# Strassen forms of the tokens through two small buffers, mix loads two tiles ahead, norms among the last products of the down stage, last up projection part by part

## The chip, the cores and the metric

The kernel runs on one core of a Trainium2 chip. The metric is the device time of one execution in microseconds (us). The engines are named as the profile names them: PE (matmul; PEld is its weight load), ACT (ScalarE), DVE (VectorE), POOL (GpSimd) and SP (SyncE, which here only issues transfers; ACT and POOL issue some too). Each engine works through its own list in order and waits on semaphores of the others.

## The reference, cut to what matters

One layer of a streaming encoder for 1024 prompt frames and 8 x 16 sample frames, all float32:

```python
x = x + 0.5 * swiglu_1(rms_norm(x, norm_ff1))    # swiglu = (silu(x @ gate) * (x @ up)) @ down
proj = rms_norm(x, norm_mix) @ w_in              # D_MODEL = 1024, D_FF = 2816
mix = concat(rwkv7(proj[rwkv columns]), band_attention(proj[attention columns]))
x = x + mix @ w_out
x = x + 0.5 * swiglu_2(rms_norm(x, norm_ff2))
y = rms_norm(x, norm_final)                      # and the recurrent states and caches
```

## The kernel before, in words

The 1152 tokens are 9 tiles of 128. Every float32 product is made of three matmuls: each operand is split into a rounded part (ACT copies it) and the rest (POOL or DVE subtracts), called hi and lo here.

**Gate and up** (both feed-forwards) use a seven-product scheme on 2 x 2 blocks. `_x_forms` makes the token side, `F`: four transposed blocks x11, x12, x21, x22 of the normalised tokens, and three further sums of them, each as hi and lo, for two parts of the tokens: part 0 is tiles 0 to 4 (2 x 320 columns), part 1 is tiles 5 to 8 (2 x 256). It goes through c = 0..3, and all of one c stands in the buffer `bs` (one of it) until POOL has made the last lo. `_w_forms` makes the weight side, `frm`: seven forms, sums `cmb` by DVE, hi by ACT, lo by POOL. `_gate_up` runs for m = 0..10 a gate pass and an up pass; a pass is seven products t = 0..6 for both parts, 12 matmuls each. After m = 0 the parts alternate within each t; for m = 0 all of part 0 runs first. The PSUM banks are reused within a pass: the products t = 0, 1, 2 are copied to SBUF by ACT (`keep`, tile `r`, 5 buffers), and t = 3, 4, 5 read such a copy on DVE (`whole`, tile `y`). The results `hs` go to DRAM.

**Down** runs for m = 0..10: load `hr` (the hidden values), split to `h`, load and split two rows of blocks of the down weights, then 9 tiles x 12 matmuls into PSUM, which DVE adds to `x`. In the first feed-forward a generator `beside` makes attention bias tables between the m, on ACT's queue and DVE. Behind it `_norm_t` normalises and transposes in three groups of three tiles, and the projection (`_project`) starts.

**Output projection** (second half of the program): `_out_proj` per tile loads `mix` and `x`, splits `mix`, runs 48 matmuls, adds to x on DVE, stores x. The token norm follows (`_rms`, then a multiply by DVE), and the forms of part 0 after tile 4, those of part 1 after tile 8; then gate and up of the second feed-forward. The order on each engine is the order in which the code emits the instructions, which a scheduler of the framework has adjusted locally; pools of SBUF and PSUM buffers set which instruction waits for which.

Of the kernel before, what the change touches and what calls it, by code (L numbers as in the profile page):

```python
# [16 lines left out]
P = 128  # L17
# [48 lines left out]
def _constants(k, a):  # L66
    nc = k.nc
    c = k.const

    def t(shape, name):  # L70
        return c.tile(shape, F32, tag=name, name=name)

    k.ident = t([P, P], "ident")
    make_identity(nc, k.ident)
    k.mhalf = t([P, 8], "mhalf")
    nc.gpsimd.memset(k.mhalf, -0.5)

    k.vec = t([P, V_N], "vec")
    _vectors(k, ((V_FF1, 8, a["norm_ff1"][0]),), nc.sync)
# [116 lines left out]
def _norm_t(k, v0):  # L196

    nc = k.nc
    for g in range(3):
        xns = []  # L200
        for i in range(3 * g, 3 * g + 3):
            xn = k.w.tile([P, DM], F32, tag="raw", bufs=k.nraw, name="xn")
# [33 lines left out]
def _x_forms(k, part, xns, v0):  # L236


    nc = k.nc
    o, n = PARTS[part]  # L240
    F = k.F[part]
    for c in range(4):
        buf = k.bsp.tile([P, 7 * 320], F32, tag="bs", bufs=1, name="bs")
        bs = buf[:, :7 * n].rearrange("p (j n) -> p j n", n=n)
        for j, cc, half in ((0, c, 0), (5, c, 1), (1, c + 4, 0), (2, c + 4, 1)):
            ps = _bank(k, "ps_n")
            t = o + half * n
            end = t + n
            while t < end:
                i, r = divmod(t, P)  # L250
                m = min(P - r, end - t)
                at = t - o - half * n
                nc.tensor.transpose(ps[:, at:at + m], xns[i - o // P][r:r + m, cc * P:cc * P + P],
                                    k.ident[r:r + m, r:r + m])
                t += m
            gain = k.vec[:, v0 + cc:v0 + cc + 1]
            if j == 5:
                nc.vector.tensor_scalar(bs[:, j], ps[:, :n], gain, None, ALU.mult)
            else:
                nc.scalar.activation(bs[:, j], ps[:, :n], AF.Copy, scale=gain)  # L260
        sub = lambda out, a, b: nc.vector.tensor_tensor(bs[:, out], bs[:, a], bs[:, b], ALU.subtract)
        sub(3, 5, 0)
        sub(4, 2, 3)
        sub(5, 2, 5)
        sub(6, 1, 4)
        nc.scalar.activation(F[:, 0, :, c], bs, AF.Copy)
        hi = F[:, 0, :, c].bitcast(F32)
        nc.vector.tensor_tensor(F[:, 1, 0:3, c], bs[:, 0:3], hi[:, 0:3], ALU.subtract)
        nc.gpsimd.tensor_tensor(F[:, 1, 3:7, c], bs[:, 3:7], hi[:, 3:7], ALU.subtract)  # L269

# [32 lines left out]
def _gate_up(k, wg, wu, hd, m):  # L303

    nc = k.nc
    hs = [k.w.tile([P, 2, 2, n], F32, tag=f"hs{p}", bufs=1, name="hs") for p, (o, n) in enumerate(PARTS)]
    for up, w in enumerate((wg, wu)):
        forms = list(_w_forms(k, w[:, 2 * m * P:2 * m * P + 2 * P]))
        state = [{}, {}]
        turns = [(t, p) for t in range(7) for p in range(2)]  # L310
        if m == 0:
            turns = [(t, p) for p in range(2) for t in range(7)]
        for t, p in turns:
# [16 lines left out]
            def keep(name):  # L330
                r = k.w.tile([P, 320], F32, tag="r", bufs=5, name="r")[:, :n]
# [3 lines left out]
            def whole(r, f, half):  # L335
                h = hs[p][:, f, half]
                y = k.w.tile([P, 320], F32, tag="y", bufs=2, name="y")[:, :n]
# [27 lines left out]

def _gate_up_pool(k, s, pool):
    k.w = pool(s, "wa")
# [3 lines left out]
def _down(k, s, pool, wd, hd, xd, done, beside=()):  # L371
# [4 lines left out]
    k.nraw = 3  # L376
    k.w = pool(s, "wb")
    k.spl = (k.w, 4)
# [3 lines left out]
    for m in range(NF // 2):  # L382
# [6 lines left out]
        d = [_load_w(k, wd[f * P:(f + 1) * P, :], [DM], None) for f in (2 * m, 2 * m + 1)]  # L389
# [4 lines left out]
        next(beside, None)  # L394
# [29 lines left out]
def _project(k, a):  # L424
# [14 lines left out]
    def shifted(c):  # L439

        wt = _cols(k, w, c * P)
# [743 lines left out]
def _out_proj(k, ws, x, xd, i):  # L1185
# [3 lines left out]
    g, j = divmod(i, 3)  # L1189
    mix = k.w.tile([P, KC, P], F32, tag="raw", bufs=k.nraw, name="mix")  # L1190
    nc.sync.dma_start(mix, k.mixd[g][:, :, j * P:j * P + P])
    nc.sync.dma_start(x, xd[i])
    s = k.mxp.tile([P, 2, KC, P], F32R, tag="mx", bufs=2, name="mx")
    nc.scalar.activation(s[:, 0], mix, AF.Copy)
    nc.vector.tensor_tensor(s[:, 1], mix, s[:, 0].bitcast(F32), ALU.subtract)
    for n in range(2):
        b = slice(512 * n, 512 * n + 512)
        ps = k.psum.tile([P, 512], F32, tag="g", name="ps_wo")
        for c in range(KC):
            mm(ps, s[:, 0, c], ws[c][:, 0, b], start=c == 0, stop=False)  # L1200
            mm(ps, s[:, 0, c], ws[c][:, 1, b], start=False, stop=False)
            mm(ps, s[:, 1, c], ws[c][:, 0, b], start=False, stop=c == KC - 1)
        nc.vector.tensor_tensor(x[:, b], ps, x[:, b], ALU.add)
    nc.sync.dma_start(xd[i], x)
# [5 lines left out]
def tile_encoder_step(ctx: ExitStack, tc: tile.TileContext, *aps):  # L1210
# [7 lines left out]
    k.nraw, k.nspl, k.nt, k.nu = 3, 4, 20, 7  # L1218
# [27 lines left out]
    with ExitStack() as s_rw, ExitStack() as s_xg:  # L1246
# [3 lines left out]
        with ExitStack() as s:  # L1250
            fp = [pool(s, f"f{p}") for p in range(2)]
            k.F = [fp[p].tile([P, 2, 7, 4, n], F32R, name="F") for p, (o, n) in enumerate(PARTS)]
            _gate_up_pool(k, s, pool)
            with ExitStack() as sb:
                k.bsp = k.h = pool(sb, "bs")
                _constants(k, a)
                for p, tiles in enumerate((range(5), range(5, 9))):
                    xns = []
# [140 lines left out]
```

## Time and profile before

| | |
|---|---|
| median of 3 runs | 2731.88 us (2724.52 to 2738.44) |
| the profiled execution | 2736.82 us, its span in the profile 2735.0 us |
| busy share of the span | PE 89%, PEld 80%, DVE 41%, ACT 33%, POOL 40% |
| clock of TensorE granted over the span | 0.937 |
| idle time of PE | 293.7 us (span less 2441.3 busy) |

In rows of a timeline the first number is the start, the second the duration of the group in us, and in brackets stands how long the engine sat idle before and what ended that. In rows of windows the numbers are the length and then the busy time of each engine. Matmul durations overlap: the pace is read from the starts.

### The profile page before, as it was taken

The page shows a single profiled execution, that of the slowest core. Times are in us where ns is not written, and L with a number is a line of the kernel's source. Part 1 is how long each engine was busy: PE and PEld are TensorE (multiplying, and loading weights), DVE is VectorE, ACT ScalarE, POOL GpSimd, SP SyncE. Part 2 cuts the span into 40 slices and gives each one's busy share as a digit, 9 for nine tenths or more (in the row PEclk, how much of TensorE's full clock was granted, in tenths as well). Part 3 has the DMA queues.
Part 4 walks back from the last instruction along what each step waited for, and adds up shares of the span by engine and source line. Part 5 has one row for each costly group of instructions (what it writes and reads, how often), then busy time and mean ns, then how long its engine had stood idle before and what let it go on. Part 6 is the DMA issues. An engine that isn't in the chain of part 4 may idle for free. (4 is left out here: it accounts for less than half of the span.)

```text
span 2735.0 us, 43547 instructions
## 1 busy us (share of the span) xinstructions
PE 2441.3 (89%) x17416; PEld 2178.8 (80%) x17416; DVE 1127.3 (41%) x2315; ACT 915.3 (33%) x1887; POOL 1093.0 (40%) x966
## 2 busy tenths in 40 slices
PE   3899999988999899999979996666699999979998
PEld 2899999976887799988856664444599999978887
DVE  4322222216555344577746554132422222215556
ACT  4333333311112344334126666121333333321112
POOL 4545454524441344334034432020555555534442
PEclk9999999988999899999969878778799999989999
DMA  2122122155222143454779853212122222243221
GB/s 100 52 77 81 64 82 64 66 181 179 98 91 80 53 136 113 118 157 159 170 177 214 199 129 100 81 31 74 43 82 64 82 64 82 64 158 125 98 91 70
DMA packets 230011, 283.70 MB, mean 104 GB/s; under 512 B 54896, under 2 KB 183536, under 8 KB 226992
## 3 DMA queue, kind: packets, MB, share of 16 engines
q1 hardware_dynamic: 196444, 233.80, 27.5%
q0 software_dynamic: 7648, 25.43, 4.0%
q10 hardware_dynamic: 25716, 21.68, 2.6%
q8 instruction: 137, 2.24, 0.4%
q14 instruction: 66, 0.54, 0.1%
HBM read 190.74 MB, written 90.12 MB: 103 GB/s over the span
## 5 line engine op out<-in xcount | busy, mean ns | idle before, releaser
L325 PE MATMUL pa<-F,frm 128*128 128x320 f32 (+1 forms) x1408 | 419.0, 298 | 23.2 <-ACT frm L283 16.9
L327 PE MATMUL pa<-F,frm 128*128 128x320 f32 (+1 forms) x1408 | 417.2, 296 | 3.4 <-POOL frm L284 3.4
L326 PE MATMUL pa<-F,frm 128*128 128x320 f32 (+1 forms) x1408 | 417.2, 296 | 0.0
L405 DVE TENSOR_TENSOR x<-pd,x 128x512 f32<-128x512 f32 x396 | 270.3, 689 | 257.9 <-PE pd L403 257.9
L164 POOL TENSOR_TENSOR spl<-raw,spl 128x1024 fp32r<-128x1024 f32 x78 | 187.1, 2401 | 434.2 <-ACT spl L163 434.1
L401 PE MATMUL pd<-spl,h 128*128 128x512 f32 x792 | 313.4, 396 | 20.8 <-ACT h L387 16.2
L326 PE MATMUL pb<-F,frm 128*128 128x256 f32 (+1 forms) x1056 | 313.8, 297 | 7.1 <-POOL F L269 5.2
L402 PE MATMUL pd<-spl,h 128*128 128x512 f32 x792 | 312.4, 394 | 6.2 <-POOL spl L164 6.2
L325 PE MATMUL pb<-F,frm 128*128 128x256 f32 (+1 forms) x1056 | 314.0, 298 | 2.5 <-ACT frm L283 2.4
L403 PE MATMUL pd<-spl,h 128*128 128x512 f32 x792 | 312.0, 394 | 3.1 <-POOL h L388 3.1
L327 PE MATMUL pb<-F,frm 128*128 128x256 f32 (+1 forms) x1056 | 313.3, 297 | 1.2 <-POOL frm L284 1.2
L284 POOL TENSOR_TENSOR frm<-cmb,frm 128x512 fp32r<-128x512 f32 x176 | 230.4, 1311 | 200.2 <-ACT frm L283 199.9
L325 PEld LDWEIGHTS pa<-F,frm 128*128 128x128 f32 x1408 | 267.6, 190 | 25.2 <-ACT frm L283 17.3
L327 PEld LDWEIGHTS pa<-F,frm 128*128 128x128 f32 x1408 | 267.6, 190 | 3.8 <-POOL frm L284 3.8
L326 PEld LDWEIGHTS pa<-F,frm 128*128 128x128 f32 x1408 | 267.6, 190 | 0.0
L284 POOL TENSOR_TENSOR frm<-raw,frm 128x512 fp32r<-128x512 f32 x132 | 173.3, 1313 | 199.2 <-ACT frm L283 197.0
L163 ACT ACTIVATE spl<-raw 128x1024 fp32r<-128x1024 f32 x78 | 82.0, 1053 | 404.1 <-issue 298.9
L326 PEld LDWEIGHTS pb<-F,frm 128*128 128x128 f32 x1056 | 201.1, 190 | 7.9 <-POOL F L269 5.7
L325 PEld LDWEIGHTS pb<-F,frm 128*128 128x128 f32 x1056 | 200.8, 190 | 3.6 <-ACT frm L283 3.3
L327 PEld LDWEIGHTS pb<-F,frm 128*128 128x128 f32 x1056 | 200.9, 190 | 1.9 <-POOL frm L284 1.9
L401 PEld LDWEIGHTS pd<-spl,h 128*128 128x128 f32 x792 | 151.5, 191 | 53.6 <-ACT h L387 16.5
L402 PEld LDWEIGHTS pd<-spl,h 128*128 128x128 f32 x792 | 151.0, 191 | 39.5 <-POOL spl L164 8.1
(258 smaller groups left out, 4647.0 us busy)
## 6 DMA issues: line engine op xcount, KB each, us to landing
raw<-in_w_ff_gate_dram SPq DMA_DIRECT2D x22, 1024.0 KB
raw<-in_w_ff_up_dram SPq DMA_DIRECT2D x22, 1024.0 KB
raw<-in_w_ff_down_dram SPq DMA_DIRECT2D x44, 512.0 KB
raw<-in_w_in_dram SPq DMA_DIRECT2D x26, 512.0 KB
hr<-hd SPq DMA_DIRECT2D x11, 1152.0 KB
hr<-he SPq DMA_DIRECT2D x11, 1152.0 KB
xd<-x SPq DMA_DIRECT2D x18, 512.0 KB
q<-qk POOLq DMA_DIRECT2D x24, 384.0 KB, 9.1
```

Source lines behind the costliest of these rows:

```text
L163: k.nc.scalar.activation(dst[:, 0], raw, AF.Copy)
L164: k.nc.gpsimd.tensor_tensor(dst[:, 1], raw, dst[:, 0].bitcast(F32), ALU.subtract)
L284: nc.gpsimd.tensor_tensor(d[:, 1], x, d[:, 0].bitcast(F32), ALU.subtract)
L325: nc.tensor.matmul(ps, frm[:, 0, c], F[:, 0, j, c], start=new and c == 0, stop=False, **kw)
L326: nc.tensor.matmul(ps, frm[:, 0, c], F[:, 1, j, c], start=False, stop=False, **kw)
L327: nc.tensor.matmul(ps, frm[:, 1, c], F[:, 0, j, c], start=False, stop=c == 3, **kw)
L401: mm(ps, h[:, 0, f, a], d[f][:, 0, b], start=f == 0, stop=False)
L402: mm(ps, h[:, 0, f, a], d[f][:, 1, b], start=False, stop=False)
L403: mm(ps, h[:, 1, f, a], d[f][:, 0, b], start=False, stop=f == 1)
L405: nc.vector.tensor_tensor(xs, ps, xs, ALU.add)
```

## The change

The parts of the change, by stage:

- **Forms.** The gain of the norm is multiplied in with the token norm (a row of gains, loaded by ACT's queue), no longer at the transposed blocks. x11, x21 and x22 go straight from PSUM to `F` (hi by ACT, lo by DVE); the buffer holds only x12 and the three sums, 4 instead of 7 columns of n. It has two buffers in the first feed-forward, one for part 0 and two for part 1 in the second.
- **Gate and up.** `r` has 4 buffers instead of 5. The up pass of m = 10 runs part by part, as m = 0 does, and its stores go on ACT's queue.
- **Down.** The weights have their own pools, so that the first ones load and split before gate and up end, with 2 instead of 3 raw buffers; the generator of the bias tables starts one m later; in the last m the norm groups 0 and 1 are emitted after tiles 4 and 7, group 2 behind it, and the first two column blocks of `w_in` are loaded and split there.
- **Output projection.** Loads of `mix` and `x` stand two tiles ahead, mixes 0 and 1 are split and half multiplied before the second half of the weights is there; the forms of part 0 come after tile 5; those of part 1 after the first weight forms of gate.
- **End.** The final norm writes into 2 instead of 3 buffers.

```diff
 def _x_forms(k, part, xns):
...
     for c in range(4):
-        buf = k.bsp.tile([P, 7 * 320], F32, tag="bs", bufs=1, name="bs")
...
+        buf = k.bsp.tile([P, k.bsw], F32, tag=k.bst, bufs=k.nbs, name="bs")
+        bs = buf[:, :4 * n].rearrange("p (j n) -> p j n", n=n)
+        x11, x12, x21, x22 = [turned(cc, half) for cc, half in ((c, 0), (c, 1), (c + 4, 0), (c + 4, 1))]
+        for j, ps in enumerate((x11, x21, x22)):
+            nc.scalar.activation(F[:, 0, j, c], ps, AF.Copy)
+            nc.vector.tensor_tensor(F[:, 1, j, c], ps, F[:, 0, j, c].bitcast(F32), ALU.subtract)
+        sub = lambda out, x, y: nc.vector.tensor_tensor(bs[:, out], x, y, ALU.subtract)
+        nc.scalar.activation(bs[:, 2], x12, AF.Copy)
+        sub(0, bs[:, 2], x11)
+        sub(1, x22, bs[:, 0])
+        sub(2, x22, bs[:, 2])
+        sub(3, x21, bs[:, 1])
+        nc.scalar.activation(F[:, 0, 3:7, c], bs, AF.Copy)
+        nc.gpsimd.tensor_tensor(F[:, 1, 3:7, c], bs, F[:, 0, 3:7, c].bitcast(F32), ALU.subtract)
...
-        if m == 0:
+        if m == 0 or (up and m == NF // 2 - 1):
             turns = [(t, p) for p in range(2) for t in range(7)]
...
-                r = k.w.tile([P, 320], F32, tag="r", bufs=5, name="r")[:, :n]
+                r = k.w.tile([P, 320], F32, tag="r", bufs=4, name="r")[:, :n]
...
-                    nc.sync.dma_start(hd[m][:, :, o:o + 2 * n], hs[p].rearrange("p f h n -> p f (h n)"))
+                    (nc.scalar if m == NF // 2 - 1 else nc.sync).dma_start(hd[m][:, :, o:o + 2 * n], hs[p].rearrange("p f h n -> p f (h n)"))
...
-        d = [_load_w(k, wd[f * P:(f + 1) * P, :], [DM], None) for f in (2 * m, 2 * m + 1)]
+        d = [_down_w(k, wd, 2 * m, k.w, 3), _down_w(k, wd, 2 * m + 1, w2, 2)]
...
-        next(beside, None)
+        if m:
+            next(beside, None)
+        if m == NF // 2 - 1 and then is not None:
+            then()
...
+            def done(i):
+                nc.scalar.dma_start(xd[i], k.x[i])
+                if i in (4, 7):
+                    next(norm)
...
+            next(norm)
+            k.first = [_cols(k, a["w_in"][0], c * P) for c in (12, 13)]
...
+            mixes = [_mix_load(k, xs[i], xd, i) for i in range(2)]
+            gain = _gain(k, a["norm_ff2"][0], k.mxp, "gain")
             ws += _out_weights(k, a["w_out"][0], range(k.nspl, KC))
             xns = []
+            split = [_mix_split(k, m) for m in mixes]
+            begun = [_out_proj(k, ws, split[i], xs[i], ((0, 4), (4, KC))) for i in range(2)]
+            for b in begun:
+                next(b)
             for i in range(NT):
...
+                if i + 2 < NT:
+                    mixes.append(_mix_load(k, xs[i + 2], xd, i + 2))
+                for _ in b:
+                    pass
+                if i + 2 < NT:
+                    split.append(_mix_split(k, mixes[i + 2]))
+                nc.sync.dma_start(xd[i], x)
...
+                if i == 5:
+                    _x_forms(k, 0, xns[:5])
...
+        k.w = pool(s, "wa")
+        forms = list(_w_forms(k, w[0][:, 0:2 * P]))
+        _x_forms(k, 1, xns[5:])
```

How it moves instructions, at three places. First SP's list in the output projection before, where L1204 stores the x of a tile and L1191 loads the next mix:

```order
L1204 DMA xd0_63<-x_17207 128x1024 [waits DMAHW4_49,DVE_49]
L1191 DMA mix_17275<-mix0_99 128x8x128 [waits DMAHW6_49,DMAHW5_49,Activation_49]
L1204 DMA xd1_64<-x_17274 128x1024 [waits DVE_49]
L1191 DMA mix_17342<-mix0_99 128x8x128 [waits DMAHW7_49,DMAHW5_49,Activation_49]
L1204 DMA xd2_65<-x_17341 128x1024 [waits DMAHW0_49,DVE_49]
```

The same list with the change (L1206 loads a mix, L1207 an x, L1412 stores an x):

```order
L1206 DMA mix_17289<-mix0_99 128x8x128 [waits DMAHW0_49,Pool_49]
L1206 DMA mix_17329<-mix1_100 128x8x128 [waits DMASW5_49,DMASW1_49,DMAHW1_49,DMASW0_49,Pool_49]
L1207 DMA x_17201<-xd7_70 128x1024 [waits DMAHW6_49]
L1412 DMA xd0_63<-x_17194 128x1024 [waits DMAHW7_49,DVE_49]
L1206 DMA mix_17369<-mix1_100 128x8x128 [waits DMAHW4_49,DVE_49]
```

Before, the load for tile 1 stands right behind the store of tile 0; now the loads for tiles 2 and 3 stand ahead of that store and the one for tile 4 right behind it.

Second, ACT's list in an up pass of the first feed-forward, from the copy of t = 1, part 1 on (L332 is `keep`, so r; L283 makes the hi of a weight form of the next pass). Before:

```order
L332 ACTIVATE r_4585<-pb_4572 128x256 [waits PE_49,Activation_49]
L283 ACTIVATE frm_4744<-cmb_4742 128x512 [waits Pool_49]
L332 ACTIVATE r_4599<-pa_4527 128x320 [waits PE_49,Activation_49]
L283 ACTIVATE frm_4749<-cmb_4747 128x512 [waits PE_49,Pool_49]
L332 ACTIVATE r_4613<-pa_4542 128x256 [waits DVE_49,Activation_49]
```

Now:

```order
L332 ACTIVATE r_4597<-pb_4584 128x256 [waits PE_49,Activation_49]
L283 ACTIVATE frm_4756<-cmb_4754 128x512 [waits Pool_49]
L283 ACTIVATE frm_4761<-cmb_4759 128x512 [waits PE_49,Pool_49]
L332 ACTIVATE r_4611<-pa_4539 128x320 [waits DVE_49,Activation_49]
L283 ACTIVATE frm_4764<-raw_4749 128x512 [waits PE_49,Pool_49]
L332 ACTIVATE r_4625<-pa_4554 128x256 [waits DVE_49,Activation_49]
```

The copy of t = 2 for part 0 (128x320 from pa) now waits for DVE too and stands behind the second form, where before it stood ahead of it and waited for PE alone.

Third, ACT's list at the start, part 0 of the forms, c = 0 to 2. Before (L260 copies a transposed block into bs, L266 makes the hi of all seven):

```order
L266 ACTIVATE F<-bs 128x7x320
L260 ACTIVATE bs<-ps_n,vec 128x320 x3
L266 ACTIVATE F<-bs 128x7x320
L260 ACTIVATE bs<-ps_n,vec 128x320 x3
L266 ACTIVATE F<-bs 128x7x320
```

Now (L260 makes the hi of one block from PSUM, L263 copies x12 to bs, L268 makes the hi of the four in bs):

```order
L263 ACTIVATE bs<-ps_n 128x320
L260 ACTIVATE F<-ps_n 128x320 x2
L268 ACTIVATE F<-bs 128x4x320
L260 ACTIVATE F<-ps_n 128x320
L263 ACTIVATE bs<-ps_n 128x320
L260 ACTIVATE F<-ps_n 128x320 x2
L268 ACTIVATE F<-bs 128x4x320
```

A copy into bs for a later c now stands ahead of the hi of the c before it; with two buffers it waits for POOL's lo of two c earlier.

More of the change, by code (lines that the diff above doesn't have):

```diff
@@ L201, in _norm_t @@
         for i in range(3 * g, 3 * g + 3):
-            xn = k.w.tile([P, DM], F32, tag="raw", bufs=k.nraw, name="xn")
+            xn = next(rooms)
             rs = _rms(k, k.x[i], xn)
@@ L241, in _x_forms @@
     F = k.F[part]
-    for c in range(4):
-        buf = k.bsp.tile([P, 7 * 320], F32, tag="bs", bufs=1, name="bs")
[L244 to L269, printed above, removed]
@@ new lines, in turned @@
+    def turned(c, half):
+        ps = _bank(k, "ps_n")
+        t = o + half * n
+        end = t + n
+        while t < end:
+            i, r = divmod(t, P)
+            m = min(P - r, end - t)
+            at = t - o - half * n
+            nc.tensor.transpose(ps[:, at:at + m], xns[i - o // P][r:r + m, c * P:c * P + P],
+                                k.ident[r:r + m, r:r + m])
+            t += m
+        return ps[:, :n]
+    for c in range(4):
+        buf = k.bsp.tile([P, k.bsw], F32, tag=k.bst, bufs=k.nbs, name="bs")
[12 more added lines that the diff above has]
+        nc.gpsimd.tensor_tensor(F[:, 1, 3:7, c], bs, F[:, 0, 3:7, c].bitcast(F32), ALU.subtract)
@@ L1195, in _out_proj @@
     nc.vector.tensor_tensor(s[:, 1], mix, s[:, 0].bitcast(F32), ALU.subtract)
+    return s
+def _out_proj(k, ws, s, x, steps=((0, KC),)):
+    nc = k.nc
+    mm = nc.tensor.matmul
+    bank = [k.psum.tile([P, 512], F32, tag="g", name="ps_wo") for n in range(2)]
+    for c0, c1 in steps:
+        for n in range(2):
+            b = slice(512 * n, 512 * n + 512)
+            ps = bank[n]
+            for c in range(c0, c1):
+                mm(ps, s[:, 0, c], ws[c][:, 0, b], start=c == 0, stop=False)
+                mm(ps, s[:, 0, c], ws[c][:, 1, b], start=False, stop=False)
+                mm(ps, s[:, 1, c], ws[c][:, 0, b], start=False, stop=c == KC - 1)
+        yield
     for n in range(2):
         b = slice(512 * n, 512 * n + 512)
[L1198 to L1204, printed above, removed]
+        nc.vector.tensor_tensor(x[:, b], bank[n], x[:, b], ALU.add)
 @with_exitstack
@@ L1269, in tile_encoder_step, with rooms, then @@
         k.xgp = pool(s_xg, "xg1", "right")
+        k.w = pool(s_xg, "w2", "right")
+        k.nraw, k.spl = 2, (k.w, 3)
         with ExitStack() as s:
-            _down(k, s, pool, w[2], hd, [x_rows(i) for i in range(NT)],
-                  lambda i: nc.sync.dma_start(xd[i], k.x[i]), _bias_tables(k, a))
             k.xg = []
-            for _ in _norm_t(k, V_MIX):
-                pass
+            norm = None
+            def rooms():
+                t = k.h.tile([P, 2 * 2 * T], F32, tag="h", bufs=2, name="xn")
+                for j in range(4):
+                    yield t[:, j * DM:(j + 1) * DM]
+                t = k.h.tile([P, 2 * T], F32, tag="hr", bufs=1, name="xn")
+                for j in range(2):
+                    yield t[:, j * DM:(j + 1) * DM]
+                t = k.h.tile([P, 2 * 2 * T], F32, tag="h", bufs=2, name="xn")
+                for j in range(4):
+                    yield t[:, j * DM:(j + 1) * DM]
+            def done(i):
+                nc.scalar.dma_start(xd[i], k.x[i])
+                if i in (4, 7):
+                    next(norm)
+            def then():
+                nonlocal norm
+                norm = _norm_t(k, V_MIX, rooms())
+            _down(k, s, pool, w[2], hd, [x_rows(i) for i in range(NT)], done, _bias_tables(k, a), then)
+            next(norm)
+            k.first = [_cols(k, a["w_in"][0], c * P) for c in (12, 13)]
         s_pr = ExitStack()
@@ L1349, in tile_encoder_step @@
             k.F.append(fp[1].tile([P, 2, 7, 4, PARTS[1][1]], F32R, name="F"))
-            _x_forms(k, 1, xns[5:], V_FF2)
-        _gate_up_pool(k, s, pool)
+            k.bsp, k.nbs, k.bsw = pool(s, "bs2", "right"), 2, 4 * PARTS[1][1]
+        k.w = pool(s, "wa")
+        forms = list(_w_forms(k, w[0][:, 0:2 * P]))
+        _x_forms(k, 1, xns[5:])
+        s_ps.close()
+        k.psum, k.ptag = pool(s, "psum_a", space=PSUM, bufs=4), "a"
         for m in range(NF // 2):
-            _gate_up(k, w[0], w[1], hd, m)
+            _gate_up(k, w[0], w[1], hd, m, forms if m == 0 else None)
     with ExitStack() as s:
```

103 lines of the change are left out of this document (58 added, 45 removed).

## The prediction

> **What bounds the kernel now.** I read the windows first, cut at the stage borders that the starts of PE's lines give. The columns of a row are the length, then the busy time of PE, PEld, DVE, ACT and POOL with their instructions, the granted clock, the DMA share and GB/s.
>
> ```profile
> 0.00:127.00 127.00, 71.98 (x405) 61.34 (x405) 57.41 (x92) 56.48 (x92) 60.61 (x46) 0.97 0.22 76
> 127.00:576.80 449.80, 449.68 (x3372) 449.49 (x3372) 111.52 (x217) 156.16 (x334) 224.42 (x199) 1.00 0.21 68
> ...
> 1694.20:1942.60 248.40, 135.82 (x515) 100.78 (x515) 61.02 (x95) 50.61 (x66) 44.50 (x24) 0.76 0.21 67
> ```
>
> Gate and up (second row) are bound by PE: it has no gap there, so any wait that the change puts in is paid in full. The other rows are the places where PE stands: 55 us in the start and 112.6 in the output projection, where no other engine is busy for more than a quarter of the time. That stage is a chain of waits, not a load; its rows came next.
>
> ```profile
> 1766.97 0.69 DVE L1203 TENSOR_TENSOR x<-ps_wo,x 128x512 f32<-128x512 f32 x1 [4.91 <-PE ps_wo L1202]
> ...
> 1768.19 0.52 SPq L1191 DMA_DIRECT2D mix<-mix  x1
> ...
> 1772.76 1.06 ACT L1194 ACTIVATE mx<-mix 128x1024 fp32r<-128x1024 f32 x1 [3.87 <-DMA mix<-mix]
> ...
> 1773.87 0.79 PE L1200 MATMUL ps_wo<-spl,mx 128*128 128x512 f32 x1 [6.94 <-ACT mx L1194]
> ...
> PE ps_wo L1200 <- ACT mx L1194: 68.4, 8, 17.9
> ```
>
> After each tile the add to x, SP's store, the load of the next mix (issued 1768.19, used 1772.76: 4.6) and its split (1.06) stand in line while PE waits 6.94; the row of waits sums eight such gaps to 68.4, the longest 17.9 at the stage's start.
>
> ```profile
> 1831.31 0.79 PE L1200 MATMUL ps_wo<-spl,mx 128*128 128x512 f32 x1 [5.86 <-ACT bs L260]
> ...
> 1832.76 0.63 PE L1200 MATMUL ps_wo<-spl,mx 128*128 128x512 f32 x1
> 1833.18 0.63 PE L1201 MATMUL ps_wo<-spl,mx 128*128 128x512 f32 x1
> ...
> 1836.09 0.39 PE L1202 MATMUL ps_wo<-spl,mx 128*128 128x512 f32 x1
> 1836.32 0.39 PE L1200 MATMUL ps_wo<-spl,mx 128*128 128x512 f32 x1
> ```
>
> After such a pause the starts are 0.43 apart for some 4.4 us, then 0.23: about 2 us more per pause.
>
> **The change part by part.** All sums stand against the profiled execution, 2736.8 us (span 2735.0), which is 0.2% above the median of the runs; the range covers that.
>
> *Output projection.* PE's need is 9 tiles x 48 matmuls x 0.233 = 11.2 each. I walk it with the new order.
>
> ```profile
> 1695.53 2.34 POOL L164 TENSOR_TENSOR spl<-raw,spl 128x1024 fp32r<-128x1024 f32 x1 [0.20 <-ACT spl L163]
> ...
> 1813.90 1.89 DVE L261 TENSOR_TENSOR bs<-bs 128x320 f32<-128x320 f32 x4
> ...
> 1824.70 2.07 ACT L266 ACTIVATE F<-bs 128x2240 fp32r<-128x2240 f32 x1 [1.42 <-DVE bs L261]
> ...
> 1826.85 3.85 POOL L269 TENSOR_TENSOR F<-bs,F 128x1280 fp32r<-128x1280 f32 x1 [4.97 <-ACT F L266]
> ...
> 1907.12 1.80 PE L253 MATMUL ps_n<-ident,x 128*128 128x128 f32 x15
> ...
> 1942.59 0.64 PE L327 MATMUL pa<-F,frm 128*128 128x320 f32 x1 [3.44 <-POOL frm L284]
> ```
>
> Attention ends at 1694.2, the window's border. Mixes 0 and 1 now land before that, so the first halves of tiles 0 and 1 start at about 1696 and run to 1709, a half-clock spell included. The last four weight blocks can load only when the mixes leave their buffers (1697): two pairs in a row, each a load of 4.6, a hi of 1.06 and POOL's 2.34, give the last lo at 1714, and both tiles end at 1724. Tiles 2 to 5 need nothing late: the load two tiles ahead has 11.2 us and takes 4.6 behind a store, the split 1.06. Tile 5 ends at 1769. The forms of part 0 have one buffer here, so a c takes POOL's 3.85, a copy of 0.5, four subtractions (1.9 and the gaps) and the hi of 1280 (1.2 by the share of 2240 in its 2.07): 7.6 for the 8.8 (3.85 and 4.97) of now. Tile 6 needs a bank that the copy of c = 2 frees, two c after the first lo at 1781.6, so at 1790; PE loses about 15 there, transposes apart. Tiles 6 to 8 end at 1825. Behind tile 8 stand add, square, power, store, multiply and transposes (6), the forms of part 1, and on POOL's queue the lo of the first weight form between them; the gate's first bank waits for the last sums: 1849.5. Before, that point was 1942.6. **Gain 92**, bounds 78 (each later step 2 us late) and 100 (POOL's queue hidden).
>
> *Gate and up, `r` with 4 buffers.*
>
> ```profile
> 340.12 0.63 ACT L283 ACTIVATE frm<-cmb 128x512 fp32r<-128x512 f32 x1 [1.00 <-PE pa L327]
> ...
> 340.83 1.29 POOL L284 TENSOR_TENSOR frm<-cmb,frm 128x512 fp32r<-128x512 f32 x1 [1.63 <-ACT frm L283]
> ...
> 342.15 0.69 DVE L289 TENSOR_TENSOR cmb<-raw 128x512 f32<-128x512 f32 x1 [2.23 <-POOL frm L284]
> 342.76 0.92 DVE L338 SCALAR_TENSOR_TENSOR y<-pb,r 128x320 f32<-128x320 f32 x2
> ...
> 343.06 0.31 PE L325 MATMUL pa<-F,frm 128*128 128x320 f32 x1
> ...
> 343.34 0.38 ACT L332 ACTIVATE r<-pa 128x256 f32<-128x256 f32 x1 [2.59 <-DVE y L338]
> ...
> ACT r L332 <- DVE y L338: 104.7, 40, 3.4
> ```
>
> Per pass six r are live until t = 3 reads the first. With five buffers only the sixth copy (343.34) waits for a y; 40 passes show that wait, and it hides behind the 1.8 us of t = 4, part 0. With four, the fifth copy waits too, and it frees the bank in which t = 4, part 0 begins. The y of t = 3 starts at 342.76, because a `cmb` of the next pass stands ahead of it on DVE and waited for POOL (340.83 + 1.29 = 342.12), which waited for the hi at 340.12, which waited for PE's own t = 2. That chain moves with PE, so it does not close up. The y takes half of its row's 0.92, the copy about 0.45 (0.38 for 256 columns): t = 4 can start at 343.7 to 343.8 instead of 343.06, 0.7 late, and queued behind it is all of PE. 19 passes in each feed-forward alternate the parts (22 less m = 0 and the last up): 38 x 0.7 to 0.8. **Loss 28**, bounds 22 and 33.
>
> *Start.*
>
> ```profile
> 51.72 3.85 POOL L269 TENSOR_TENSOR F<-bs,F 128x1280 fp32r<-128x1280 f32 x1 [1.48 <-ACT F L266]
> ...
> 86.19 3.19 POOL L269 TENSOR_TENSOR F<-bs,F 128x1024 fp32r<-128x1024 f32 x1 [5.11 <-ACT F L266]
> ```
>
> A c takes 8.8 here too, without other work between. Two buffers put only a copy (0.5), two direct copies (1.0) and the hi (1.2) between two lo of POOL: 6.6, and 5.4 for part 1. Against seven such steps (about 16) stands a start some 3 us later: a load of gains, and a norm multiply with two operands (1.28 in the final norm's row, below). The last lo of part 0 comes at about 43 for 51.7, that of part 1 at 72 to 75 for 86.2. **Gain 14**, bounds 9 and 18.
>
> *Down 1, both ends.*
>
> ```profile
> 617.97 2.22 ACT L387 ACTIVATE h<-hr 128x1152 fp32r<-128x1152 f32 x2 [26.73 <-DVE bias L150]
> ...
> 673.25 0.69 DVE L405 TENSOR_TENSOR x<-pd,x 128x512 f32<-128x512 f32 x1 [0.71 <-PE pd L403]
> 674.61 0.69 DVE L405 TENSOR_TENSOR x<-pd,x 128x512 f32<-128x512 f32 x1 [0.67 <-PE pd L403]
> ...
> 879.78 2.78 PE L210 MATMUL ps_n<-ident,xn 128*128 128x128 f32 x24
> ...
> 902.64 4.29 DVE L213 SCALAR_TENSOR_TENSOR xg<-ps_n,vec,xg 128x384 fp32r<-128x384 f32 x8 [1.18 <-ACT xg L212]
> ...
> 911.93 0.69 PE L228 MATMUL ps_p<-xg,spl 128*128 128x384 f32 x1 [2.65 <-POOL spl L164]
> ```
>
> Steady, an m takes 18 x 1.36 = 24.5, so 11 take 269.3 of the 303.0 between 576.8 and 879.78: 33.7 over. ACT's split of the second h stood 26.73 behind the tables; it is done ahead of them now. But POOL has a lo of h (5.2) ahead of the weights', and the load of hr waits for the last stores. I take 23 to 24 over, **gain 10**, bounds 5 and 14. Then norm to projection took 32.2 (879.78 to 911.93). Now group 2 alone follows: square, power and multiply of its tiles (4.6), transposes and the eight lo of 4.29 (13.2 in all), with 6.6 of transposes moved into the last m: 19.8. **Gain 12**, bounds 8 and 14.
>
> *Second down and end.*
>
> ```profile
> 2457.16 0.69 DVE L405 TENSOR_TENSOR x<-pd,x 128x512 f32<-128x512 f32 x1 [19.76 <-PE pd L403]
> ...
> 2725.35 1.28 DVE L1358 SCALAR_TENSOR_TENSOR y<-x,ss,gain 128x1024 f32<-128x1024 f32 x1
> ...
> 2727.96 1.28 DVE L1358 SCALAR_TENSOR_TENSOR y<-x,ss,gain 128x1024 f32<-128x1024 f32 x1
> ```
>
> The first add comes 19.76 after the last pass; early weights shorten it, the gain row and two x loads ahead of hr keep most of it. **Gain 3**, bounds 1 and 6. The last tiles are 2.61 apart; with two buffers a square waits for the store of two tiles before; with the multiply (1.28), a store of some 3 us and the next square and power that makes 6 per two tiles, an estimate, for seven tiles. **Loss 3**, bounds 2 and 6.
>
> **Sum:** 2736.8 - 92 - 14 - 10 - 12 - 3 + 28 + 3 = **2637**. All small bounds together give 2675, all large ones 2609.
>
> **The rivals.** *The stall of r costs nothing* (10%): if DVE takes y ahead of the `cmb`, t = 4 starts on time: 2637 - 28 = 2609. For it speaks that PE is done with that product 1.4 us (12 matmuls of part 1) before 343.06; against it the order on DVE, which has the `cmb` first.
>
> *The output projection stays in the grip of its loads* (10%): mix loads stand behind stores that wait for adds, and if each tile still costs half of its pause, 92 becomes about 47: 2682. Against it: 4.6 us of load in 11.2 of matmuls.
>
> *PE's clock falls in gate and up* (4%), the case that ends slower. Two pauses per pass, before t = 4 of each part, would each start a spell at half clock like the one at 1831.31: 2 x 2.2 more in 38 passes is 167, so 2804. It decides from 2.6 us per pass on. What the trace has on short pauses:
>
> ```profile
> 1972.83 0.41 PE L325 MATMUL pa<-F,frm 128*128 128x320 f32 x1 [0.53 <-ACT r L332]
> ...
> 1973.23 0.31 PE L327 MATMUL pa<-F,frm 128*128 128x320 f32 x1
> 1973.37 0.31 PE L325 MATMUL pa<-F,frm 128*128 128x320 f32 x1
> ```
>
> One wait of the very kind, 0.53 long, and 0.15 per matmul behind it: no spell. The Trainium skill, "TensorE: Matmul & The Clock Gate", section "A second HAM failure mode: psum-queue depth-cycling", tells of a kernel whose PE paused briefly between groups of matmuls as it cycled its PSUM banks, and whose clock swung between half and full rate; that is the shape of these passes, and by it this rival would hold. The single pause of this trace speaks against it; a train of them no row shows.
>
> *Nothing on the path moves* (3%): 2737, if the tiles' waits are only renamed.
>
> **How the numbers follow.** The forecast has 70%, the remaining 3% lie outside. 0.5% (13.7 us) is about what a measurement of this kernel tells from no change. The range 2602 to 2688 takes in the bounds and the two middle rivals. Faster 0.94, same 0.02, slower 0.04.
>
> **What would show it.** In the windows: PE idle in the output projection falls from 112 to under 30 and the stage to about 155 us; ACT's mx no longer releases PE there. In gate and up: PE idle about 0.7 per pass, released by ACT's r, with twice as many waits of r for y. POOL's F rows at the start 6.6 apart. Norm to projection near 20. I am wrong if gate and up keep their period of 22.4, or if PE's clock there falls below 1.00, or if the tiles stay more than 13 us apart.

## The result, and the profile after

The changed kernel takes 2650.45 us (median of 4 runs, 2645.15 to 2656.27) against 2730.99 in the same session for the kernel before (4 runs, 2724.52 to 2738.44): a ratio of 0.9705, 95% interval 0.9672 to 0.9737. The profiled execution took 2648.95, its span is 2647.2, which is 87.8 less than the 2735.0 before.

The windows of the changed kernel, cut at its own stage borders (columns as in the prediction):

```profile
0.00:114.00 114.00, 70.98 (x405) 59.56 (x405) 55.63 (x99) 52.07 (x100) 58.58 (x46) 1.00 0.26 89
114.00:580.50 466.50, 454.60 (x3372) 450.54 (x3372) 111.29 (x216) 156.33 (x336) 226.57 (x199) 1.00 0.21 69
580.50:905.60 325.10, 292.86 (x1262) 235.38 (x1263) 163.31 (x266) 68.27 (x87) 128.62 (x90) 0.94 0.39 134
905.60:1677.80 772.20, 719.43 (x6982) 609.41 (x6982) 442.42 (x1190) 350.77 (x872) 267.11 (x338) 0.93 0.57 146
1677.80:1835.10 157.30, 122.86 (x513) 94.52 (x513) 67.19 (x107) 45.87 (x78) 42.34 (x27) 0.86 0.31 106
1835.10:2346.40 511.30, 495.81 (x3696) 491.13 (x3696) 124.76 (x235) 173.50 (x371) 250.85 (x216) 1.00 0.21 69
2346.40:2647.20 300.80, 272.85 (x1188) 224.44 (x1188) 148.83 (x218) 54.12 (x60) 112.64 (x55) 0.96 0.30 112
```

The rows of the kernel before for the stretches that the prediction doesn't show:

```profile
576.80:911.90 335.10, 294.65 (x1265) 240.18 (x1264) 175.95 (x271) 68.83 (x88) 124.92 (x88) 0.92 0.38 131
911.90:1694.20 782.30, 724.33 (x6979) 611.53 (x6979) 440.75 (x1185) 351.80 (x872) 271.41 (x340) 0.92 0.56 146
...
1942.60:2436.90 494.30, 491.48 (x3694) 490.65 (x3694) 132.38 (x240) 175.52 (x373) 251.92 (x219) 0.99 0.21 68
2436.90:2735.00 298.10, 273.36 (x1189) 224.79 (x1188) 148.31 (x217) 55.89 (x62) 115.27 (x53) 0.96 0.33 120
```

Read row against row, the first column gives the account: start 13.0 less, first gate/up 16.7 more, first down with its norm 10.0 less, projections and attention 10.1 less, output projection 91.1 less, second gate/up 17.0 more, second down and end 2.7 more. Together 87.8. One difference of cut is in these numbers: at 911.9 and 1942.6 the kernel before is cut where the third product of the projection and of the gate stops waiting for the lo of its weights (their first products are at 908.3 and 1938.2), while the changed kernel has no such wait and is cut at the first product. Cut at the first product in both, first down is 6.4 less, projections and attention 13.7 less, output projection 86.7 less and second gate/up 12.6 more.

The row of waits that carried the prediction, `ps_wo` released by ACT's `mx` with 68.4 in 8 gaps, is down to one wait of 1.8. PE's largest groups of waits are now:

```profile
PE pa L325 <- ACT r L332: 25.5, 39, 1.4
PE pd L418 <- ACT spl L162: 17.6, 2, 16.9
PE ps_n L250 <- ACT bs L263: 17.6, 9, 4.5
```

The first is new: 39 waits of 0.65 in 38 passes. One of them in order of time:

```profile
314.59 0.91 DVE L338 SCALAR_TENSOR_TENSOR y<-pb,r 128x320 f32<-128x320 f32 x2
...
314.76 0.28 PE L327 MATMUL pb<-F,frm 128*128 128x256 f32 x1
315.17 0.44 ACT L332 ACTIVATE r<-pa 128x320 f32<-128x320 f32 x1 [2.59 <-DVE y L338]
...
315.66 0.42 PE L325 MATMUL pa<-F,frm 128*128 128x320 f32 x1 [0.62 <-ACT r L332]
...
315.91 0.31 PE L326 MATMUL pa<-F,frm 128*128 128x320 f32 x1
```

The fifth copy of a pass (t = 2, part 0) has no buffer until DVE has made the first y of t = 3; it starts at 315.17, and t = 4 of part 0 needs the PSUM bank that it reads. PE would have gone on at 314.88 (its spacing is 0.12 here) and starts at 315.66, 0.78 late; the next matmul comes 0.25 behind instead of 0.147, 0.10 more. That is 0.88 a pass, and the windows give (16.7 + 17.0) / 38 = 0.89. The granted clock is 1.00 in both gate/up rows.

In the output projection the tiles run at PE's own pace. Two splits of mixes, and a mix load between them:

```profile
1742.87 1.06 ACT L1214 ACTIVATE mx<-mix 128x1024 fp32r<-128x1024 f32 x1 [9.10 <-PE ps_wo L1231]
...
1745.21 0.52 SPq L1206 DMA_DIRECT2D mix<-mix  x1
...
1754.06 1.06 ACT L1214 ACTIVATE mx<-mix 128x1024 fp32r<-128x1024 f32 x1 [9.10 <-PE ps_wo L1231]
```

They are 11.19 apart, and ACT now waits for PE (9.10) where PE waited for ACT. PE still stands 34.4 of the stage's 157.3 (length less busy time), a little more than the 30 that the prediction allowed.

### The profile page after: what moved, and what is told of

It is laid out like the page before. It is cut to its first block, busy times and chain, and to the rows that moved or that the text cites. A ratio compares the mean times of both kernels' runs of the same rounds, so it can differ in the third digit from the quotient of the medians.

```text
span 2647.2 us, 43489 instructions
## 1 busy us (share of the span) xinstructions
PE 2429.4 (92%) x17415; PEld 2165.0 (82%) x17415; DVE 1113.4 (42%) x2330; ACT 900.9 (34%) x1903; POOL 1086.7 (41%) x966
## 5 line engine op out<-in xcount | busy, mean ns | idle before, releaser
L325 PE MATMUL pa<-F,frm 128*128 128x256 f32 (+1 forms) x1408 | 422.3, 300 | 44.6 <-ACT r L332 25.5
L327 PE MATMUL pa<-F,frm 128*128 128x256 f32 (+1 forms) x1408 | 416.8, 296 | 0.0
L326 PE MATMUL pa<-F,frm 128*128 128x256 f32 (+1 forms) x1408 | 416.8, 296 | 0.0
L327 PE MATMUL pb<-F,frm 128*128 128x320 f32 (+1 forms) x1056 | 312.7, 296 | 4.0 <-POOL frm L284 4.0
L325 PE MATMUL pb<-F,frm 128*128 128x320 f32 (+1 forms) x1056 | 313.6, 297 | 2.5 <-ACT frm L283 2.5
L326 PE MATMUL pb<-F,frm 128*128 128x320 f32 (+1 forms) x1056 | 312.9, 296 | 2.4 <-POOL F L269 2.4
```

The source lines that it names most:

```text
L325: nc.tensor.matmul(ps, frm[:, 0, c], F[:, 0, j, c], start=new and c == 0, stop=False, **kw)
L326: nc.tensor.matmul(ps, frm[:, 0, c], F[:, 1, j, c], start=False, stop=False, **kw)
L327: nc.tensor.matmul(ps, frm[:, 1, c], F[:, 0, j, c], start=False, stop=c == 3, **kw)
```

## The experiments

Every experiment is a kernel with its own trace, read by stage; stage borders are the first and last matmul of a stage. All but the fifth, which follows the third here because it answers it, are built on the changed kernel. Where a time comes from one run alone, the text says so, and the verdict rests on the trace.

**1. The copy u2 in the y buffers.** Two y tiles are taken once per feed-forward, and the copy of t = 2 goes into columns that y leaves free:

```diff
+        k.turn, k.y2 = 0, [k.hx.tile([P, k.ny], F32, tag="y", bufs=2, name="y") for _ in range(2)]
 ...
-                r = k.w.tile([P, 320], F32, tag="r", bufs=4, name="r")[:, :n]
+                if name == "u2":
+                    r = k.y2[p][:, 320:320 + n]
+                else:
+                    r = k.w.tile([P, 320], F32, tag="r", bufs=4, name="r")[:, :n]
 ...
-                y = k.hx.tile([P, k.ny], F32, tag="y", bufs=2, name="y")[:, :n]
+                y = k.y2[k.turn % 2][:, :n]
+                k.turn += 1
```

> The copy u2 goes into unused columns of the two y buffers, so that the four r buffers serve four copies a pass-half instead of six; nothing else changes. Theory (the stall is the wait of the fifth copy for the first y): the passes go back from 23.27 to 22.40 us in the first gate/up and from 23.09 to 22.19 in the second, 38 passes x 0.87 to 0.90 = 34 less, 2650 to about 2616; the row of PE's idle time released by ACT's r (25.5 us in 39 gaps) is gone. Rival (PE stands for something else, such as the wider y buffers or the forms): the passes stay at 23.27 and 23.09 and the time at 2650.

Measured: 2614.33 (2612.06 to 2618.07), ratio to the kernel before 0.9561 (0.9533 to 0.9589). Its gate/up windows, and what is left of the waits for r:

```profile
114.00:564.30 450.30, 449.90 (x3372) 449.54 (x3372) 110.25 (x218) 158.57 (x337) 228.44 (x199) 1.00 0.22 72
1815.70:2310.20 494.50, 491.62 (x3696) 490.61 (x3696) 122.75 (x235) 175.82 (x371) 252.12 (x216) 0.99 0.22 72
```

```profile
PE pa L327 <- ACT r L337: 1.0, 2, 0.5
```

466.5 falls to 450.3 and 511.3 to 494.5, the same matmuls in the same time as before the change (449.8 and 494.3). The stall is the missing room for the fifth copy, and its price is 33 (by these rows) to 36 (by the times).

**2. A pad of 32 bytes.** The spacing of matmuls in the first down had gone from 0.227 to 0.231 at a granted clock of 1.00. The change had moved one of the two weight blocks (the moving operand, 512 columns) to the right side of SBUF, where the buffers start 32 bytes off a multiple of 64. The places are those of the pools' layout in the built kernels; the traces hold no addresses.

```diff
+    pool(ctx, "pad", "right").tile([P, 8], F32, name="pad")
     with ExitStack() as s_rw, ExitStack() as s_xg:
```

> A pad of 32 bytes per partition at the top of the right side; every buffer on the right moves down by 32 bytes and then starts at a multiple of 64, nothing else changes. Theory (a matmul whose moving operand starts 32 bytes off a multiple of 64 takes longer): the spacing in the first down falls from 0.231 to 0.227 (an m from 24.95 to 24.48, 5 us in all), in the output projection from 0.2333 to 0.227 (432 x 0.0066 = 3 us), in the projections by perhaps 2% of 0.1735: 2650 to about 2640. Rival (the distance of the operands, or the upper half of the memory, makes them slow): all spacings stay, 2650.

Measured: 2645.25 (2639.45 to 2648.80), ratio 0.9666 (0.9631 to 0.9700), whose interval overlaps that of the changed kernel. The spacing answers the pad exactly. In the output projection of the changed kernel (first fence) and of this one (second), two matmuls of one uninterrupted row that are 11 apart:

```profile
1734.73 0.39 PE L1231 MATMUL ps_wo<-spl,mx 128*128 128x512 f32 x1
...
1737.30 0.40 PE L1230 MATMUL ps_wo<-spl,mx 128*128 128x512 f32 x1
```

```profile
1734.69 0.39 PE L1229 MATMUL ps_wo<-spl,mx 128*128 128x512 f32 x1
...
1737.18 0.39 PE L1231 MATMUL ps_wo<-spl,mx 128*128 128x512 f32 x1
```

2.57 / 11 = 0.234 becomes 2.49 / 11 = 0.226; the first down goes to 0.227 as well, and the projections (384 columns) stay at 0.1735. But the second gate/up got longer, and the first down did not get shorter:

```profile
580.60:908.50 327.90, 290.43 (x1263) 236.94 (x1263) 165.58 (x266) 68.16 (x87) 128.45 (x90) 0.93 0.38 133
...
1830.50:2345.90 515.40, 500.92 (x3696) 496.30 (x3696) 125.02 (x235) 173.59 (x371) 251.12 (x216) 0.99 0.21 69
```

```profile
PE pd L418 <- DVE x L422: 5.5, 2, 3.0
```

515.4 against 511.3: the forms of part 1 (256 columns) lay 32 off there and now lie at a multiple of 64, and their spacing went from 0.117 to 0.120. And 327.9 against 325.1: PE, faster by about 5 in the steady blocks, waited 5.5 for late x loads near the start (the changed kernel waits 1.83 there).

**3. Mix loads not ahead.**

```diff
-            mixes = [_mix_load(k, xs[i], xd, i) for i in range(2)]
 ...
             for i in range(NT):
                 x = xs[i]
-                ...
+                for _ in _out_proj(k, ws, _mix_split(k, _mix_load(k, x, xd, i)), x):
+                    pass
```

> Output projection: each tile's mix is loaded and split at its own turn, behind the store of the tile before, and no products of tiles 0 and 1 are begun early. Theory (the gain of that stage is the load that moved ahead): eight gaps of about 7 us and one of 18 at the stage's start come back, 68 as in the kernel before, less some 2 to 4 that the norm's new place gives: 2650 to about 2715, the tiles 18 apart for 11.2. Rival (the gain came from the forms of part 0, the early gate weights and the two buffers of the forms): under 20 more, 2670 at most.

Measured: 2675.6 (one run), 25 more than the changed kernel and not 65. Attention (first row) and output projection (second), and the only wait for a mix:

```profile
908.90:1693.50 784.60, 723.62 (x6982) 612.35 (x6982) 440.81 (x1190) 350.96 (x871) 266.71 (x338) 0.92 0.56 144
1693.50:1861.80 168.30, 119.97 (x514) 92.88 (x513) 67.33 (x107) 45.95 (x78) 42.17 (x27) 0.84 0.30 99
```

```profile
PE ps_wo L1229 <- ACT mx L1214: 18.2, 1, 18.2
```

The wait at the stage's start came back; those between tiles did not (seven of them, since one of the eight gaps in the old row is the 17.9 at the start). So what the code says about loading ahead is not what freed the tiles. SP's list of this kernel shows why: the framework's scheduler has put the loads ahead of the stores by itself, four of them ahead of the first store. Both theories fail, the first by most of its size. And attention became 12.4 longer (784.6 against 772.2), which neither had.

**5. One line of the kernel before.** What else had the change done there? In the kernel before the square of a finished tile wrote its scratch into a `raw` buffer, and mixes use the same two buffers. So the old kernel was run with another place for the scratch and nothing else:

```diff
-                rs = _rms(k, x, k.w.tile([P, DM], F32, tag="raw", bufs=k.nraw, name="junk"))
+                junk = k.bsp.tile([P, 7 * 320], F32, tag="bs", bufs=1, name="junk")
+                rs = _rms(k, x, junk[:, :DM])
```

> The kernel before, with one line changed: the scratch tile of each tile's square in the output projection no longer takes a raw buffer (it takes the forms' buffer), so that the two raw buffers hold mixes alone. No load is written earlier in the code. Theory (a mix waited for the raw buffer of the square before it, and goes ahead by itself once that is gone): of the gaps on ACT's mx eight of 6 to 7 us go and the one of 18 at the stage's start stays, with the half-clock spells behind them: 50 to 60 less, 2732 to about 2675. Rival (the mixes move only where the code loads them two tiles ahead): tiles stay 18 apart, 2732.

Measured: 2673.17 (one run) against 2735.34 for the kernel before in that session. Its output projection and its largest waits:

```profile
1698.70:1875.50 176.80, 120.50 (x512) 93.93 (x512) 58.19 (x93) 49.67 (x65) 40.22 (x22) 0.82 0.27 94
```

```profile
PE ps_n L253 <- ACT bs L260: 40.1, 7, 7.6
...
PE ps_wo L1200 <- ACT mx L1194: 16.8, 1, 16.8
```

This window ends at the gate's first product. The row of before, 248.4, ran on to the third product, which waits here just as it did there:

```profile
1879.88 0.63 PE L327 MATMUL pa<-F,frm 128*128 128x320 f32 x1 [3.45 <-POOL frm L284]
```

On the same cut 248.4 falls to 181.2, 67.2 less by one line. A piece of SP's list in this kernel, where in the kernel before every load of a mix (L1191) but the first stands behind a store (L1204):

```
L1191 DMA mix<-mix_99 128x8x128 x2
L1192 DMA x<-xd_67 128x1024
L1192 DMA x<-xd_68 128x1024
L1191 DMA mix<-mix_99 128x8x128
L1191 DMA mix<-mix_100 128x8x128
```

Four mixes now stand ahead of the first store, though the code still asks for each at its own tile. Of the 91.1 of this stage 67.2 are the scratch's buffer. By experiment 3 the early mixes are worth another 11.0 (168.3 to 157.3). The rest, 12.9, is left for the new forms, their buffers and the early gate weights, which weren't tried apart; 4.4 of it is the way from the gate's first to its third product.

**4. The norm behind the last product.**

```diff
             def done(i):
                 nc.scalar.dma_start(xd[i], k.x[i])
-                if i in (4, 7):
-                    next(norm)
 ...
-            next(norm)
+            for _ in range(3):
+                next(norm)
```

> All three groups of the norm stand behind the last product of the first down, instead of two among the products. Theory (the two groups among the products are worth the time between the last product and the projection): that time grows from 15 to about 32 us as before the change, the last m gets shorter by some 6 for the transposes: net 12 more, 2662. Rival (only the last group's own chain sets the end): under 4 more.

Measured: 2642.62 (one run). First gate/up's end to the first projection:

```profile
580.40:904.50 324.10, 292.86 (x1264) 235.55 (x1263) 164.04 (x266) 68.42 (x87) 129.13 (x90) 0.94 0.38 135
```

324.1 against 325.1: transposing two groups among the products gains nothing, and the 12 that the theory expected did not come. The transposes of both groups follow the last product in one go, and the multiplies that feed them had run among the products all the same:

```profile
877.98 0.76 DVE L203 TENSOR_SCALAR xn<-x,ss 128x1024 f32<-128x1024 f32 x1 [0.66 <-POOL ss L187]
...
881.92 6.28 PE L209 MATMUL ps_n<-ident,xn 128*128 128x128 f32 x48
...
904.42 0.29 PE L451 MATMUL ps_st<-ident,st 112*128 112x112 f32 x1 [2.88 <-DMA st<-in_state_shift_dram]
```

From the last product (881.7) to the projection's first matmul are 22.7, where the kernel before took 28.6 and the changed one takes 14.9; but in the changed one the last product comes at 890.6, 8.9 later. The place of the transposes only moves time. What shortens the way from 28.6 to 22.7 in this experiment is probably that the normalised tiles have ten places in the hidden values' buffers instead of three raw buffers; that wasn't tried apart.

**6. u2 in y, with pads chosen by stage.** Built on experiment 1.

```diff
+        pool(s_xg, "pad1", "right").tile([P, 8], F32, name="pad")
         k.xgp = pool(s_xg, "xg1", "right")
 ...
+        pool(s3, "pad3", "right").tile([P, 8], F32, name="pad")
         k.w = pool(s3, "w3", "right")
 ...
+            pool(s, "pad0").tile([P, 8], F32, name="pad")
             fp = [pool(s, f"f{p}") for p in range(2)]
+            pool(s, "pad2").tile([P, 8], F32, name="pad")
```

> Built on the kernel with u2 in the y buffers (2614). Pads of 32 bytes: the buffers of the first down, the projections and the output projection start at multiples of 64, those of part 1's forms in the second gate/up stay 32 off; in the first gate/up both parts' forms are put 32 off (weights' forms stay at multiples of 64). Theory (512 columns want a multiple of 64, 256 columns an offset of 32, 320 columns don't care): m of the first down 24.95 to 24.48 (-5), output projection -3, first gate/up from 22.40 to 22.19 a pass (-4), second unchanged: about 2602. Rival (320 columns behave as 512, 3% longer when 32 off): first gate/up 22.19 + 84 x 0.0044 = 22.56 a pass, about 2609. Rival (256 columns gain from the distance of the two parts' forms and not from the offset): first gate/up stays at 22.40, 2606.

Measured: 2608.84 (2603.74 to 2615.64), ratio 0.9553 (0.9510 to 0.9596); by the times alone it can't be told from experiment 1. By stage:

```profile
114.00:560.90 446.90, 446.88 (x3372) 446.68 (x3372) 109.85 (x216) 158.45 (x336) 226.66 (x198) 1.00 0.22 72
1807.60:2302.00 494.40, 491.59 (x3696) 490.68 (x3696) 122.71 (x235) 175.77 (x371) 252.31 (x215) 0.99 0.22 72
```

The first gate/up falls from 450.3 to 446.9 (a steady pass from 22.40 to 22.26, where the theory had 22.19), the second stays. The forms 32 off are better for 256 columns, and 320 columns are at most slightly worse; both rivals fail. The output projection's matmuls take 125.0 from first to last for 128.5. The first down gave its pace back again: one wait of 2.94 for x.

**7. Three small ends.**

```diff
-            k.bsp, k.bst, k.nbs, k.bsw = k.hx, "y", 2, k.ny
+            k.bsp, k.bst, k.nbs, k.bsw = pool(s, "b1"), "bs", 1, k.ny
 ...
-    nc.scalar.dma_start(extd, ext)
+    nc.sync.dma_start(extd, ext)
 ...
-        k.w = pool(s, "w4")
+        k.w, k.nraw = pool(s, "w4"), 3
```

> Three edits, each read in its own stage. First: the forms of tokens at the start go through one buffer of their own instead of two. If the two buffers are worth the gain of the start, the first copy of pass 2 comes some 8 to 10 later than 94.8; if it is the norm's gain row, or the copies from PSUM straight to the forms, under 3. Second: the 12 KB store of the bias generator goes out from SP's queue instead of ACT's, so that ACT's first split of weights no longer stands behind it: the first product of the first down comes up to 4 earlier than 597.4; if the weights' own load is late, it stays. Third: three buffers instead of two for the last tiles' outputs: the time from the last product to the end falls from 12.7 to about 9. Together about 2653.

Measured: 2645.69 (one run). The last lo of the forms of part 0 and of part 1 at the start in the changed kernel (first fence), and that of part 1 in this one (second):

```profile
47.27 2.88 POOL L269 TENSOR_TENSOR F<-bs,F 128x1280 fp32r<-128x1280 f32 x1
...
74.74 2.84 POOL L269 TENSOR_TENSOR F<-bs,F 128x1024 fp32r<-128x1024 f32 x1
```

```profile
81.57 2.34 POOL L269 TENSOR_TENSOR F<-bs,F 128x1024 fp32r<-128x1024 f32 x1 [2.72 <-ACT F L268]
```

With one buffer the last lo comes 6.8 later, the first copy of pass 2 comes 7.3 later (102.1 for 94.8, less than the 8 to 10 expected), and the last product of the first gate/up 7.4 later (587.6 for 580.2). So the second buffer is worth about 7 of the start's 13; the other 6 come with the copies straight from PSUM and the gain row, which weren't taken apart.

The store on SP's queue: the first product of the first down stands 14.8 behind the last up, for 16.9, and its split now waits for its own load:

```profile
601.54 2.15 ACT L162 ACTIVATE spl<-raw 128x1024 fp32r<-128x1024 f32 x2 [2.15 <-DMA raw<-in_w_ff_down_dram]
```

The wait for x didn't come either, and the whole stretch to the projection is 319.0 for 325.1. With three output buffers the last squares no longer wait for a store, and the time from the last product's start to the end is 8.3 for 12.7.

**8. The four gains together**: experiment 6 with the last two edits of experiment 7.

> The four edits that gained in their own stages, together: u2 in the y buffers, the pads, the bias generator's store on SP's queue, three buffers for the last outputs. If they add up: 2609 (u2 and pads) - 6 (from the end of the first gate/up to the projection) - 4 (last product to end) = about 2599. If the start of the first down is paid again in another wait (late x loads, as when the pads were put in), 2605.

Measured: 2598.76 (5 runs, 2590.80 to 2600.51), ratio to the kernel before 0.9493 (0.9471 to 0.9514): they add up, and this is 52 less than the changed kernel.

## Why the prediction was right, and where it was not

The forecast was 2637 with a range of 2602 to 2688; 2650.45 lies in it, 13 above the forecast. The four large terms have the forecast sign, two of them another size, and two of the reasons were wrong. That the sum comes so near is partly luck: first down fell 12 short of its gain, and projections and attention, which were not in the sum, gave 10. The measured column uses the rows above as they are cut there, which is also the cut of the prediction's terms.

| Term | Forecast | Measured |
|---|---|---|
| Output projection | -92 | -91.1 |
| Start | -14 | -13.0 |
| First down and its norm | -22 | -10.0 |
| Second down and end | 0 (-3 and +3) | +2.7 |
| r with four buffers | +28 | +33.7 |
| Projections, attention | 0 | -10.1 |

**Output projection.** The size was right, the cause only in part. The prediction read that the add, the store, the load and the split stood in line, and gave the gain to the code that loads ahead. The walk held tile by tile: counted from the end of attention, the last product of the second tile was forecast at 29.8 and came at 31.0, that of the sixth at 74.8 and 75.8, that of the ninth at 130.8 and 131.2, the gate's first at 155.3 and 157.3. But experiments 3 and 5 show that the line was held by the scratch of the square, which took turns with the mixes in two buffers: without it the scheduler moves the loads up by itself, in the old code too, and that is 67.2 of the 91.1. The early loads are needed only for the 18 at the stage's start (and they come with the 12 of attention, below). What I had in hand was enough to see it: the change also moves the scratch from a `raw` buffer to the forms' buffer, a line that the list of its parts above leaves out. The rival in which half of each pause stays is refuted by the 11.19 between two splits.

**Start.** Forecast were the last lo of part 0 at about 43 and that of part 1 at 72 to 75; they come at 47.27 and 74.74 (experiment 7), for 51.72 and 86.19. So part 0 was 4 late, its rows of POOL 6.9 to 9.0 apart and not 6.6, and part 1 on time.

**r with four buffers.** The mechanism is shown by experiment 1, which gives both stages their old time back. The size was short: the term took the pause alone, 0.7 to 0.8; the delay is 0.78 and the first matmul after a pause costs 0.10 more, which puts 33.7 just outside the term's bounds of 22 and 33. The rival in which the stall costs nothing is refuted by the same rows. One detail was wrong: that twice as many copies would wait for a y. Before there were 40 (104.7 us, in the prediction), and now there are about as many:

```profile
ACT r L332 <- DVE y L338: 97.7, 38, 3.3
```

It was the sixth copy that waited then, with a product in between before its bank was needed; now it is the fifth, whose bank PE needs next. About the same count and length, another place behind it.

**The clock.** The rival that ends slower needed two pauses per pass, each starting a spell at half clock. There was one per pass, and 39 pauses of 0.65 in 38 passes left the granted clock at 1.00 in both gate/up rows. The Trainium skill's page "TensorE: Matmul & The Clock Gate", section "A second HAM failure mode: psum-queue depth-cycling", describes a bf16 kernel with 512 columns in which frequent short idling between groups of matmuls makes the clock swing; this trace doesn't show that for pauses of this length and rate.

**First down.** This is the term that failed. Its gain of 10 at the start was booked on ACT's split of the second h going ahead of the bias tables. It did (589.28), but the weights' split came next to stand behind the same tables, and the first product came 17.2 behind the last one of gate and up, where the kernel before took 12.8:

```profile
589.28 2.22 ACT L401 ACTIVATE h<-hr 128x1152 fp32r<-128x1152 f32 x2 [10.72 <-DMA hr<-hd]
...
593.47 2.39 DVE L124 TENSOR_SCALAR room<-room 8x257 f32<-8x257 f32 x1 [12.52 <-DMA room<-in_rel_bias_dram]
595.89 0.28 ACTq L126 DMA_DIRECT2D ext_d<-room  x1
596.27 1.06 ACT L162 ACTIVATE spl<-raw 128x1024 fp32r<-128x1024 f32 x1 [4.77 <-DVE room L124]
597.38 0.50 PEld L418 LDWEIGHTS pd<-spl,h 128*128 128x128 f32 x2 [17.09 <-ACT spl L162]
```

ACT holds the split behind the issue of a 12 KB store, which waits for DVE, which waits for a small load. Experiment 7 takes that store away and gets 6 of the stretch; the split then waits for the weights' own load. The list of the change's parts says that the first weights load and split before gate and up end. In the first feed-forward they don't: on SP's queue they stand behind the load of the second hr, which waits 5.6 for POOL's lo of the first h:

```profile
583.54 0.34 SPq L398 DMA_DIRECT2D hr<-hd  x1
583.94 0.42 SPq L407 DMA_DIRECT2D x<-in_x_prompt_dram  x1
584.46 1.40 SPq L380 DMA_DIRECT2D raw<-in_w_ff_down_dram  x2
```

That is 4.3 behind the last product of gate and up (580.2); the kernel before issued its first one at 575.4, ahead of that product (576.5). What this order costs was not tried. Another 5 went into the pace, since the steady block of an m took 24.95 for 24.48: the working took the old row's duration for matmuls whose operand the change had moved (experiment 2). With the transposes in the last m taken out, 0.6 of the 10 is left. The 12 of the norm came out at 9.4: from the last product to the first one of the projection (905.6) are 15.1 for the forecast 13.2, and the last m is 8.0 longer than in experiment 4 for the forecast 6.6. The reason was wrong besides: transposes among the products only put the same work before the last product instead of behind it (experiment 4).

**Projections and attention** were held for untouched. They aren't: the scheduler places attention's instructions by what follows them. On one basis, from the first projection product to attention's end, the kernel before:

```profile
908.30:1694.20 785.90, 725.31 (x6982) 612.00 (x6982) 441.59 (x1190) 351.80 (x872) 274.93 (x350) 0.92 0.56 145
```

On this basis the changed kernel takes 772.2. Matched product by product, the two are within 1 us of each other 615 us after the first projection product, so nearly all of the 13.7 arises in the last 160 us of attention. Experiments 3 and 5, with the first mixes late, take 784.6 and 788.0; the changed kernel and experiments 2 and 4, with them early, 772.2, 769.1 and 769.8. The two groups don't overlap, and in experiment 3 PE's list departs from the changed kernel's among attention's score and output products, well ahead of the output projection. That the order makes the difference is likely by this, but no run held everything but the order fixed.

**Second down and the end.** The early weights gave 1.4 for the forecast 3. The end cost 4.0 for the forecast 3, and for the forecast reason: with two output buffers the squares of the last tiles wait for stores,

```profile
2640.20 1.06 ACT L185 ACTIVATE y<-x 128x1024 f32<-128x1024 f32 x1 [2.05 <-DMA out_dram<-y]
```

and a third buffer (experiment 7) takes it away.

## What to carry to other kernels

A scratch tile that shares its buffers with a prefetched operand can set the order of the loads, whatever the code says about loading ahead: look at which tiles take turns in a tag before rewriting the loop. When a buffer is taken from a rotating set, count which use waits next and what engine stands right behind it, since the same number of waits can cost nothing in one place and a pause per pass in the next. Where a framework's scheduler makes the lists, a stage that the diff doesn't touch can still change, so a blind sum should leave room for it.

## What the runs showed of the hardware

At a granted clock of 1.00 the pace of matmuls depends on where the moving operand starts. With 512 columns of this type a start at a multiple of 64 bytes gives 0.226 to 0.227 us from matmul to matmul, 32 bytes beyond one 0.234 (output projection), 0.231 where one of two alternating operands lies so (first down). With 256 columns it is the other way round: 0.120 at a multiple of 64 and 0.117 off it (0.118 on the mean where the 320 columns of the other part lie off it too, experiment 6). With 384 columns there is no difference (0.1735). A pad of 32 bytes switches between them (experiments 2 and 6); the starts are those of the pools' layout, and the cause of the opposite signs stays open. The Trainium skill's page "TensorE: Matmul & The Clock Gate", section "Back-to-back issue gap", gives the gap of an isolated matmul as columns / 2.4 + 2.5 ns, 216 ns for 512, and a sustained 131 ns for a stream of weight loads and matmuls; both paces here, 226 and 234 ns in such a stream, are longer than either.
